# RMSNorm with swish, 16 x 1024 x 512 in fp32: in-place fp32 tiles in a deep pool, a Silu table, and stores issued from ScalarE

## The chip, the cores and the metric

The kernel runs on one core of a Trainium2 chip; the other cores are idle. The metric is device time in microseconds (us), the median over runs. A verdict of "faster" or "slower" needs a difference clear of 2%.

Engines: VectorE (DVE in the profile), ScalarE (ACT), GpSimd (POOL), SyncE (SP), and the DMA engines. `ACTq` or `SPq` is the sequencer of an engine: the part that takes instructions in order, waits for semaphores and issues DMA transfers.

## The reference

```python
# x: (16, 1024, 512) fp32, gamma: ones(512), eps: 1e-5
rms = np.sqrt(np.mean(x ** 2, axis=-1, keepdims=True) + eps)
x_norm = x / rms * gamma
return x_norm * (1.0 / (1.0 + np.exp(-x_norm)))
```

There are 16,384 rows, cut into 32 tiles of 128 partitions x 4 rows x 512 columns. A tile is 1 MiB in and 1 MiB out.

## The kernel before

Five stages of different tiles are written per step: load, squares, statistics and normalisation, sigmoid, multiply and store. A scheduler then fixes each engine's order and the semaphores.

```python
xpool = ctx.enter_context(tc.tile_pool(name="xin", bufs=6))
ypool = ctx.enter_context(tc.tile_pool(name="ybuf", bufs=5))
opool = ctx.enter_context(tc.tile_pool(name="obuf", bufs=5))
# ... load: SyncE
nc.sync.dma_start(out=x_t[:], in_=xv[t])
# ... squares: three rows on ScalarE, the fourth on VectorE; sums into ms
# ... statistics and normalisation
nc.vector.tensor_scalar_add(out=aeps[:], in0=ms[:], scalar1=eps_f)
nc.gpsimd.tensor_tensor(out=rstd[:], in0=aeps[:], in1=neg_half[:], op=ALU.pow)
for j in range(n):                          # n = 4; y is bf16
    nc.vector.scalar_tensor_tensor(out=y[:, j, :], in0=x_t[:, j, :],
        scalar=rstd[:, j : j + 1], in1=gamma_sb[:], op0=ALU.mult, op1=ALU.mult)
# ... sigmoid on ScalarE, multiply on VectorE, store from GpSimd (bf16 to fp32)
nc.scalar.activation(out=o[:], in_=y[:], func=AF.Sigmoid)
nc.vector.tensor_tensor(out=o[:], in0=y[:], in1=o[:], op=ALU.mult)
nc.gpsimd.dma_start(out=ov[t], in_=o[:])
```

## Time and profile before

| | before |
|---|---|
| time, median of 3 | 189.42 us (187.84 to 190.24) |
| DMA | 67.42 MB, mean 360 GB/s, best slices 430 |
| VectorE busy per tile | 145.1 / 32 = 4.5 us |
| ScalarE busy per tile | 122.6 / 32 = 3.8 us |

These are lines of the profile's first page for the kernel before. Part 1 gives busy time and share of the span. Part 2 cuts the span into 40 slices of 4.7 us; a digit is the busy share in tenths.

```profile
span 187.5 us, 803 instructions
## 1 busy us (share of the span) xinstructions
DVE 145.1 (77%) x257; ACT 122.6 (65%) x226; POOL 56.8 (30%) x68
## 2 busy tenths in 40 slices
DVE  0168999966998579987489976689965789999930
ACT  2478999945994289973199872399737299744520
...
DMA  6999999999999969999959999969999969887484
GB/s 171 366 421 432 367 369 418 419 426 407 388 378 402 432 257 341 395 425 423 430 231 385 383 430 421 414 231 397 383 426 425 411 199 402 318 306 285 192 309 170
```

Read the last row first. Where the DMA has work queued it moves about 425 GB/s. At that rate 67.42 MB take 159 us, so the span holds about 29 us in which the DMA was not full. The holes are of two kinds. In the first 130 us single slices drop to 257, 231 and 231 GB/s. In the last 28 us (six slices) the rate stays between 170 and 320 GB/s, while VectorE shows 9 until two slices from the end.

The next view groups instructions by line; after the bar come busy us and mean ns of one.

```profile
L105 DVE SCALAR_TENSOR_TENSOR y<-x_t,rstd,gamma_sb 128x512 bf16<-128x512 f32 x128 | 87.4, 744 | 2.3 <-POOL rstd L100 2.3
L118 ACT ACTIVATE o<-y 128x2048 bf16<-128x2048 bf16 x32 | 60.5, 1902 | 11.4 <-DVE y L105 11.1
...
L124 DVE TENSOR_TENSOR o<-y,o 128x2048 bf16<-128x2048 bf16 x32 | 39.0, 1219 | 10.4 <-ACT o L118 10.4
```

VectorE pays 4 x 744 ns for the normalisation of a tile and 1219 ns for the multiply. The waits of SyncE's DMA queue say why loads came late: a load waits until VectorE has normalised the tile that held its buffer.

```profile
engine line waited for: us in total, times, longest us
SPq L64 <- DVE y L105: 139.3, 26, 10.9
```

### The profile page before, as it was taken

How to read it: one execution, taken by the hardware profiler on the slowest of the kernel's cores; microseconds unless marked ns; L12 is line 12 of the kernel's file. 1: busy time of each engine (PE TensorE's matmuls, PEld its weight loads, DVE VectorE, ACT ScalarE, POOL GpSimd, SP SyncE). 2: the span in 40 equal slices, each digit the busy share in tenths (PEclk: the TensorE clock that was granted, in tenths of full speed). 3: DMA queues.
4: the chain of work that ended last, by engine and by line, in shares of the span. 5: the costliest groups of instructions: out<-in, count | busy, mean ns of one | idle time of the engine just before them, and what ended most of it. 6: DMA issues, size and time to landing. Idle time of an engine off the chain costs nothing.

```text
span 187.5 us, 803 instructions
## 1 busy us (share of the span) xinstructions
DVE 145.1 (77%) x257; ACT 122.6 (65%) x226; POOL 56.8 (30%) x68
## 2 busy tenths in 40 slices
DVE  0168999966998579987489976689965789999930
ACT  2478999945994289973199872399737299744520
POOL 0022651542117701236402145402132802146120
DMA  6999999999999969999959999969999969887484
GB/s 171 366 421 432 367 369 418 419 426 407 388 378 402 432 257 341 395 425 423 430 231 385 383 430 421 414 231 397 383 426 425 411 199 402 318 306 285 192 309 170
DMA packets 9365, 67.42 MB, mean 360 GB/s; under 512 B 1040, under 2 KB 1040, under 8 KB 1168
## 3 DMA queue, kind: packets, MB, share of 16 engines
q1 hardware_dynamic: 4608, 33.56, 53.6%
q0 software_dynamic: 4608, 33.56, 46.7%
q10 hardware_dynamic: 144, 0.26, 0.5%
q14 instruction: 5, 0.04, 0.1%
HBM read 33.82 MB, written 33.55 MB: 359 GB/s over the span
## 4 chain that ended last, share of the span: by engine, by line
DMA 35%; DVE 25%; issue 20%; ACT 8%; POOL 7%; POOLq 0%; SPq 0%; ACTq 0%; DVEq 0%
DMA x_t<-in_x_dram 35%; DVE y L105 19%; POOL rstd L100 5%; DVE o L124 5%; ACT o L118 5%; ACT junk_act L74 4%; POOL out_dram L125 2%; DVE junk_dve L82 1%; DVE aeps L98 0%; POOLq L174 0%; SPq L64 0%; DVE ms L82 0%; POOLq L125 0%; ACTq L74 0%; ACTq L118 0%
## 5 line engine op out<-in xcount | busy, mean ns | idle before, releaser
L105 DVE SCALAR_TENSOR_TENSOR y<-x_t,rstd,gamma_sb 128x512 bf16<-128x512 f32 x128 | 87.4, 744 | 2.3 <-POOL rstd L100 2.3
L74 ACT ACTIVATE junk_act<-x_t 128x512 bf16<-128x512 f32 x96 | 59.1, 616 | 44.2 <-DMA x_t<-in_x_dram 44.2
L118 ACT ACTIVATE o<-y 128x2048 bf16<-128x2048 bf16 x32 | 60.5, 1902 | 11.4 <-DVE y L105 11.1
L125 POOL DMA_DIRECT2D out_dram<-o x32 | 18.0, 563 | 100.3 <-DVE o L124 66.8
L124 DVE TENSOR_TENSOR o<-y,o 128x2048 bf16<-128x2048 bf16 x32 | 39.0, 1219 | 10.4 <-ACT o L118 10.4
L100 POOL TENSOR_TENSOR rstd<-aeps,neg_half 128x4 f32<-128x4 f32 x32 | 38.6, 1214 | 24.0 <-DVE aeps L98 23.7
L82 DVE CUSTOM_DVE_ANT_0 junk_dve<-x_t 128x512 bf16<-128x512 f32 x32 | 21.4, 686 | 22.0 <-DMA x_t<-in_x_dram 22.0
L74 ACT ACTIVATION_READ_ACCUMULATOR junk_act<-x_t 128x1 f32 x96 | 17.9, 187 | 0.0
L98 DVE TENSOR_SCALAR aeps<-ms 128x4 f32<-128x4 f32 x32 | 4.3, 160 | 0.0
L82 DVE DVE_READ_ACCUMULATOR2_ANT ms<- 128x1 f32 x32 | 2.6, 81 | 0.0
L74 ACT ACT_TABLE_LOAD x1 | 1.3, 1283 | 1.2 <-PEq L160 1.2
L118 ACT ACT_TABLE_LOAD x1 | 1.3, 1283 | 0.0
L50 DVE MEMSET neg_half<- 128x4 f32 x1 | 0.1, 62 | 0.8 <-PEq L160 0.8
L160 POOL MEMSET const-float32-0.0<- 128x1 f32 x1 | 0.1, 99 | 0.2 <-issue 0.2
L160 POOL MEMSET const-bfloat16-1.0<- 128x1 bf16 x1 | 0.1, 102 | 0.0
L160 POOL MEMSET const-uint8-127<- 128x1 uint8 x1 | 0.1, 102 | 0.0
L160 POOL MEMSET const-float32-1.0<- 128x1 f32 x1 | 0.1, 99 | 0.0
## 6 DMA issues: line engine op xcount, KB each, us to landing
x_t<-in_x_dram SPq DMA_DIRECT2D x32, 1024.0 KB, 8.5
out_dram<-o POOLq DMA_DIRECT2D x32, 1024.0 KB, 9.0
gamma_sb<-in_gamma_dram ACTq DMA_DIRECT2D x1, 256.0 KB, 6.8
```

The lines of the kernel that those rows point to most:

```text
L50: nc.vector.memset(neg_half[:], -0.5)
L74: nc.scalar.activation(out=junk_act[:, j, :], in_=x_t[:, j, :], func=AF.Square, scale=inv_sqrt_d, accum_out=ms[:, j : j + 1],)
L82: nc.vector.tensor_tensor_reduce(out=junk_dve[:, j - n_act_sq, :], in0=x_t[:, j, :], in1=x_t[:, j, :], scale=inv_d, scalar=0.0, op0=ALU.mu ...
L98: nc.vector.tensor_scalar_add(out=aeps[:], in0=ms[:], scalar1=eps_f)
L100: nc.gpsimd.tensor_tensor(out=rstd[:], in0=aeps[:], in1=neg_half[:], op=ALU.pow)
L105: nc.vector.scalar_tensor_tensor(out=y[:, j, :], in0=x_t[:, j, :], scalar=rstd[:, j : j + 1], in1=gamma_sb[:], op0=ALU.mult, op1=ALU.mult,)
L118: nc.scalar.activation(out=o[:], in_=y[:], func=AF.Sigmoid)
L124: nc.vector.tensor_tensor(out=o[:], in0=y[:], in1=o[:], op=ALU.mult)
L125: nc.gpsimd.dma_start(out=ov[t], in_=o[:])
L160: nc = _bacc.Bacc("TRN2", target_bir_lowering=False, num_devices=1)
```

## The change

The intent: keep one fp32 tile from load to store and work in place, which takes away the bf16 copies; replace sigmoid and multiply by one Silu on ScalarE, which takes 39 us from VectorE; give the tiles 20 buffers so that loads never wait; issue stores from ScalarE, right behind the Silu that they store. The core of the diff, with imports, asserts, renamings, the scratch pools, the squares (their scale by 1/512 moves into the statistics instruction) and the start of the load loop cut:

```diff
-    xpool = ctx.enter_context(tc.tile_pool(name="xin", bufs=6))
-    ypool = ctx.enter_context(tc.tile_pool(name="ybuf", bufs=5))
-    opool = ctx.enter_context(tc.tile_pool(name="obuf", bufs=5))
+    lead = 10
+    xpool = ctx.enter_context(tc.tile_pool(name="xbuf", bufs=20))
+    nc.scalar.preload_act_table_set("silu_and_others")
 ...
-        nc.vector.tensor_scalar_add(out=aeps[:], in0=ms[:], scalar1=eps_f)
+        nc.vector.tensor_scalar(
+            out=aeps[:], in0=ms[:], scalar1=inv_d, scalar2=eps_f,
+            op0=ALU.mult, op1=ALU.add,
+        )
 ...
-                out=y[:, j, :], in0=x_t[:, j, :], ...
+                out=x_t[:, j, :], in0=x_t[:, j, :], ...
 ...
-        nc.scalar.activation(out=o[:], in_=y[:], func=AF.Sigmoid)
-        nc.vector.tensor_tensor(out=o[:], in0=y[:], in1=o[:], op=ALU.mult)
-        nc.gpsimd.dma_start(out=ov[t], in_=o[:])
+        nc.scalar.activation(out=x_t[:], in_=x_t[:], func=AF.Silu)
+        nc.scalar.dma_start(out=ov[t], in_=xt.pop(t)[:])
 ...
+    for k in range(T + 3):
+        if k < T:
+            stats(k)
+            rstd(k)
+        if 0 <= k - 1 < T:
+            norm(k - 1)
+        if 0 <= k - 2 < T:
+            swish(k - 2)
+            store(k - 2)
+        if k + lead < T:
+            load(k + lead)
```

More of the change, by code (lines that the diff above doesn't have):

```diff
@@ L1 @@
-import math
 from contextlib import ExitStack
@@ L5 @@
 import concourse.tile as tile
-from concourse import bass_utils, mybir
+from concourse import mybir
 from concourse._compat import with_exitstack
@@ L30 @@
     n = 4
-    n_act_sq = 3 if n >= 4 else n
-    rows_per_tile = P * n
-    assert R % rows_per_tile == 0, (R, rows_per_tile)
-    T = R // rows_per_tile
+    n_act = 3
+    lead = 10
+    T = R // (P * n)
+    assert T * P * n == R, (R, n)
     xv = xf.rearrange("(t p n) d -> t p n d", p=P, n=n)
@@ L39, with load, stats @@
     consts = ctx.enter_context(tc.tile_pool(name="consts", bufs=1))
-    xpool = ctx.enter_context(tc.tile_pool(name="xin", bufs=6))
-    ypool = ctx.enter_context(tc.tile_pool(name="ybuf", bufs=5))
-    opool = ctx.enter_context(tc.tile_pool(name="obuf", bufs=5))
-    junk_pool = ctx.enter_context(tc.tile_pool(name="junk", bufs=3))
+    xpool = ctx.enter_context(tc.tile_pool(name="xbuf", bufs=20))
+    junk_a = ctx.enter_context(tc.tile_pool(name="junk_a", bufs=2))
+    junk_v = ctx.enter_context(tc.tile_pool(name="junk_v", bufs=2))
     small = ctx.enter_context(tc.tile_pool(name="small", bufs=6))
+    nc.scalar.preload_act_table_set("silu_and_others")
     gamma_sb = consts.tile([P, D], fp32)
-    nc.scalar.dma_start(out=gamma_sb[:], in_=gamma.partition_broadcast(P))
     neg_half = consts.tile([P, n], fp32)
     nc.vector.memset(neg_half[:], -0.5)
-    inv_sqrt_d = 1.0 / math.sqrt(float(D))
     inv_d = 1.0 / float(D)
     eps_f = float(eps)
-    x_tiles: dict[int, bass.AP] = {}
-    ms_tiles: dict[int, bass.AP] = {}
-    rstd_tiles: dict[int, bass.AP] = {}
-    y_tiles: dict[int, bass.AP] = {}
-    o_tiles: dict[int, bass.AP] = {}
-    def stage_load(t):
+    xt: dict[int, bass.AP] = {}
+    ms_of: dict[int, bass.AP] = {}
+    rstd_of: dict[int, bass.AP] = {}
+    def load(t):
         x_t = xpool.tile([P, n, D], fp32, name="x_t")
         nc.sync.dma_start(out=x_t[:], in_=xv[t])
-        x_tiles[t] = x_t
-    def stage_sq(t):
-        x_t = x_tiles[t]
+        xt[t] = x_t
+    def stats(t):
+        x_t = xt[t]
         ms = small.tile([P, n], fp32, name="ms")
-        junk_act = junk_pool.tile([P, n_act_sq, D], bf16, name="junk_act")
-        junk_dve = junk_pool.tile([P, max(1, n - n_act_sq), D], bf16, name="junk_dve")
         for j in range(n):
-            if j < n_act_sq:
+            if j < n_act:
+                junk = junk_a.tile([P, D], bf16, name="sq_act")
                 nc.scalar.activation(
-                    out=junk_act[:, j, :],
-                    in_=x_t[:, j, :],
-                    func=AF.Square,
-                    scale=inv_sqrt_d,
+                    out=junk[:], in_=x_t[:, j, :], func=AF.Square,
                     accum_out=ms[:, j : j + 1],
@@ L81, in stage_sq @@
             else:
+                junk = junk_v.tile([P, D], bf16, name="sq_dve")
                 nc.vector.tensor_tensor_reduce(
-                    out=junk_dve[:, j - n_act_sq, :],
-                    in0=x_t[:, j, :],
-                    in1=x_t[:, j, :],
-                    scale=inv_d,
-                    scalar=0.0,
-                    op0=ALU.mult,
-                    op1=ALU.add,
+                    out=junk[:], in0=x_t[:, j, :], in1=x_t[:, j, :],
+                    scale=1.0, scalar=0.0, op0=ALU.mult, op1=ALU.add,
@@ L90, in stage_sq, with rstd @@
                     accum_out=ms[:, j : j + 1],
                 )
-        ms_tiles[t] = ms
-    def stage_rstd_y(t):
-        ms = ms_tiles.pop(t)
-        x_t = x_tiles.pop(t)
+        ms_of[t] = ms
+    def rstd(t):
+        ms = ms_of.pop(t)
         aeps = small.tile([P, n], fp32, name="aeps")
-        nc.vector.tensor_scalar_add(out=aeps[:], in0=ms[:], scalar1=eps_f)
-        rstd = small.tile([P, n], fp32, name="rstd")
-        nc.gpsimd.tensor_tensor(
-            out=rstd[:], in0=aeps[:], in1=neg_half[:], op=ALU.pow
-        )
-        y = ypool.tile([P, n, D], bf16, name="y")
+        nc.vector.tensor_scalar(
+            out=aeps[:], in0=ms[:], scalar1=inv_d, scalar2=eps_f,
+            op0=ALU.mult, op1=ALU.add,
+        )
+        r = small.tile([P, n], fp32, name="rstd")
+        nc.gpsimd.tensor_tensor(out=r[:], in0=aeps[:], in1=neg_half[:], op=ALU.pow)
+        rstd_of[t] = r
@@ L104, in stage_rstd_y, with norm @@
+    def norm(t):
+        x_t = xt[t]
+        r = rstd_of.pop(t)
         for j in range(n):
             nc.vector.scalar_tensor_tensor(
-                out=y[:, j, :],
-                in0=x_t[:, j, :],
-                scalar=rstd[:, j : j + 1],
-                in1=gamma_sb[:],
-                op0=ALU.mult,
-                op1=ALU.mult,
-            )
-        y_tiles[t] = y
-    def stage_sigmoid(t):
-        y = y_tiles[t]
-        o = opool.tile([P, n, D], bf16, name="o")
-        nc.scalar.activation(out=o[:], in_=y[:], func=AF.Sigmoid)
-        o_tiles[t] = o
@@ L121, in stage_out @@
-    def stage_out(t):
-        y = y_tiles.pop(t)
-        o = o_tiles.pop(t)
-        nc.vector.tensor_tensor(out=o[:], in0=y[:], in1=o[:], op=ALU.mult)
-        nc.gpsimd.dma_start(out=ov[t], in_=o[:])
-    NS = 5
-    for k in range(T + NS - 1):
-        t_out = k - 4
-        t_sig = k - 3
-        t_y = k - 2
-        t_sq = k - 1
-        t_ld = k
-        if 0 <= t_out < T:
-            stage_out(t_out)
-        if 0 <= t_sig < T:
-            stage_sigmoid(t_sig)
-        if 0 <= t_y < T:
-            stage_rstd_y(t_y)
-        if 0 <= t_sq < T:
-            stage_sq(t_sq)
-        if 0 <= t_ld < T:
-            stage_load(t_ld)
+                out=x_t[:, j, :], in0=x_t[:, j, :], scalar=r[:, j : j + 1],
@@ new lines, in norm, with swish, store @@
+                in1=gamma_sb[:], op0=ALU.mult, op1=ALU.mult,
+            )
+    def swish(t):
+        x_t = xt[t]
+        nc.scalar.activation(out=x_t[:], in_=x_t[:], func=AF.Silu)
+    def store(t):
+        nc.scalar.dma_start(out=ov[t], in_=xt.pop(t)[:])
+    load(0)
+    nc.scalar.dma_start(out=gamma_sb[:], in_=gamma.partition_broadcast(P))
+    for t in range(1, lead):
+        load(t)
+    for k in range(T + 3):
[9 more added lines that the diff above has]
+            load(k + lead)
```

## The prediction

> **What bounds the kernel before.** No single engine. The DMA row of the profile moves 67.42 MB in a 187.5 us span, mean 360 GB/s; its good slices reach 418 to 432. At 425 GB/s the traffic alone would take 159 us (an estimate), so about 29 us are DMA slack. It is lost in two places. First, in the slices near 66, 94 and 122 us the rate falls to 199 to 257 GB/s: the SyncE queue waited 139 us in total for the VectorE normalisation to free one of six load buffers (view of waits), and the loads then come in bursts that start compute again (chain of waits: four DMA pieces of 9.6 to 12.4 us). Second, from 143 us on all loads are in or nearly in and VectorE is 9 to 10 tenths busy at about 3.8 us a tile, while the DMA falls to 170 to 320 GB/s. VectorE's work per tile is 4.5 us (145.1/32): 4 x 744 ns, 1219 ns multiply, 686+81+160 ns.
>
> **What the change does.** VectorE loses the 1219 ns multiply: about 3.45 us a tile (normalisation start to start is 0.66 us where undisturbed). ScalarE: sigmoid becomes Silu of the same 2048 elements. The Trainium skill (ScalarE: Activation LUTs, "What ACT_TABLE_LOAD costs") says one element per cycle for every function, fp32 and bf16 alike; the trace agrees on the step (616 ns for 512 fp32, 1902 ns for 2048 bf16: 0.84 ns an element). So 3 x 0.614 + 1.83 = 3.7 us a tile, and ScalarE becomes the slower compute engine. One table load of 1.28 us goes. Stores leave GpSimd (18 us of issue there, not critical); an issue from the SyncE queue takes 0.42 us, mostly hidden under the next square on ScalarE. The DMA bytes are unchanged; the skill (DMA: Bandwidth & Descriptors, "Issuing engines are not separate DMA queues") says the same 16 engines serve all queues, so the floor of 159 us stays.
>
> **What I expect to bind.** The built order of the changed kernel shows that loads and stores now share eight completion semaphores in turn, each transfer waiting for the one eight places before. So store 5 waits for load 10, store 7 for load 14, store 9 for load 19, store 14 for load 27, and this wait sits in ScalarE's instruction stream: ScalarE is held until loads run far ahead. Phase 1: DMA full, two loads to each store, to store 14: about 41.5 transfers of 2.47 us from 7.4 us on, i.e. until about 106 us. Phase 2: loads nearly done, 17 tiles of compute left at 3.7 us on ScalarE: about 64 us, DMA only about 0.8 full. Then the last store, 4 to 6 us. Span about 173 us; time about 173.5 us, 8 times in 10 within 164 to 180. Faster by over 2%: 0.94; within 2%: 0.05; slower: 0.01.
>
> **What would show it.** DMA slices at 410 to 430 GB/s without dips to about 100 us, then 270 to 350 until the end; ScalarE idle in the first half with store issues waiting for loads of x, and 9 to 10 tenths busy in the last third; VectorE about 112 us busy in all; GpSimd about 40 us; the chain ending in ScalarE and a store rather than VectorE.
>
> **What would make it wrong.** If the shared semaphores don't hold ScalarE, DMA stays full throughout: 161 to 165 us. If the store issue stalls ScalarE by its full 0.42 us and more, phase 2 grows by 8 us or more. If fp32 stores and loads mixed on two hardware queues run below 425 GB/s, phase 1 grows.

## The result and the profile after

| | before | after |
|---|---|---|
| time, median of 4 runs | 188.63 us (187.78 to 190.24) | 185.50 us (185.32 to 185.71) |
| ratio, 95% interval | | 0.9896 (0.9863 to 0.9929): the same within 2% |
| span | 187.5 us | 183.7 us |
| VectorE busy | 145.1 us | 110.7 us |

Ratios in the experiments differ from the ratio of the medians by at most 0.002. For the change the listed medians give 0.983, and 0.9896 can't be worked out again from the runs listed; by either figure the change is worth less than 2%.

The time lies outside the predicted 164 to 180 us, on the slow side. VectorE's busy time fell by 34 us and the time by 3. The slices of the changed kernel are 4.6 us each:

```profile
span 183.7 us, 711 instructions
...
DVE 110.7 (60%) x225; ACT 120.9 (66%) x225; POOL 32.8 (18%) x36
...
DVE  0177877777725527064443777777777777777650
ACT  2449988842572643168076987999988888888450
...
DMA  5999999999999999999999999999985555555195
GB/s 178 338 428 428 425 426 428 423 426 426 428 425 426 423 426 428 425 426 428 428 426 428 428 426 428 428 425 426 425 359 234 228 228 228 228 228 228 57 400 230
```

The DMA row has two parts. From the third to the 29th slice, to about 133 us, it is full at about 425 GB/s without a hole, as hoped. For the last ten, from about 138 us, it carries mostly 228 GB/s. That is one 1 MiB store per 4.6 us (1.049 MB / 4.62 us = 227 GB/s): all loads are done and the stores come at the pace of the computation. Within the full stretch, from the ninth to the 22nd slice, ScalarE falls again and again to between 0 and 4 tenths, and VectorE with it. They are held back there, and are short of time later.

What held them is seen in ScalarE's timeline. The columns are start, duration, engine, line and operation; the bracket is the engine's idle time before and what the profile holds to have ended it.

```profile
start us, us, engine line op out<-in xcount [idle before <-releaser]
...
69.80 0.61 ACT L68 ACTIVATE sq_act<-x_t 128x512 bf16<-128x512 f32 x1
...
76.83 0.34 ACTq L106 DMA_DIRECT2D out_dram<-x_t  x1
77.21 0.63 ACT L68 ACTIVATE sq_act<-x_t 128x512 bf16<-128x512 f32 x1 [6.71 <-DMA x_t<-in_x_dram]
...
77.84 0.61 ACT L68 ACTIVATE sq_act<-x_t 128x512 bf16<-128x512 f32 x1
```

The first square of a tile runs at 69.80 us, so that tile has landed. The second square of the same tile starts 6.71 us late, right behind the issue of a store (76.83 us). The bracket names a load, but it can't be this tile's own. It is the store's wait: the built order of the changed kernel has for this store (the store of tile 9, its tile named x_t_93)

```
58 L68 Activation sq_act_340,ms_339<-x_t_148 128x512 [waits Activation_49]
59 L106 DMACopy out_0_dram<-x_t_93 128x2048 [waits DMAHW3_49,Activation_49]
```

and semaphore DMAHW3 was last given to the load of tile 19. In the trace that load lands at 76.75 us, and the store is issued at 76.83 us. The same holds for eleven stores (4 to 12, 14 and 15): each is issued 0.07 to 0.08 us after the landing of the load that had its semaphore before. Loads from SyncE and stores from ScalarE take eight completion semaphores in turn, and a transfer waits for the one that had its semaphore before. The Trainium skill (DMA: Bandwidth & Descriptors, "Anatomy of one DMA — SWDGE (gpsimd) path") says, in a section on transfers from GpSimd: "DMA engines do not wait on semaphores", and that a wait happens on the issuing sequencer before dispatch. This trace of stores from ScalarE agrees: the wait shows as idle ScalarE. The first line below puts 41.9 us of it down to loads, 13 times. Two of these, 6.2 us at the start, are waits for a tile's own load; the other eleven, 35.7 us, are the held stores.

```profile
ACT sq_act L68 <- DMA x_t<-in_x_dram: 41.9, 13, 6.7
DVE x_t L96 <- POOL rstd L89: 37.4, 32, 1.2
```

The second line is the other loss: VectorE waits for GpSimd once per tile, 32 times, 37.4 us. The timeline of VectorE and GpSimd shows it, from 103 us on:

```profile
103.56 0.68 DVE L74 CUSTOM_DVE_ANT_0 sq_dve<-x_t 128x512 bf16<-128x512 f32 x1
...
104.17 0.17 DVE L84 TENSOR_SCALAR aeps<-ms 128x4 f32<-128x4 f32 x1
104.48 1.01 POOL L89 TENSOR_TENSOR rstd<-aeps,neg_half 128x4 f32<-128x4 f32 x1 [3.61 <-DVE aeps L84]
...
105.53 2.74 DVE L96 SCALAR_TENSOR_TENSOR x_t<-x_t,rstd,gamma_sb 128x512 f32<-128x512 f32 x4 [1.19 <-POOL rstd L89]
...
108.18 0.68 DVE L74 CUSTOM_DVE_ANT_0 sq_dve<-x_t 128x512 bf16<-128x512 f32 x1
```

One tile after another, VectorE computes the statistics of a tile (L84), GpSimd raises them to the power (L89, 1.01 us), and only then VectorE normalises the same tile (L96). It idles 1.19 us each time, and square to square the period is 108.18 - 103.56 = 4.62 us. It keeps this period to the last square at 168 us. The costs of single instructions are what the prediction took:

```profile
L96 DVE SCALAR_TENSOR_TENSOR x_t<-x_t,rstd,gamma_sb 128x512 f32<-128x512 f32 x128 | 87.8, 747 | 37.4 <-POOL rstd L89 37.4
L103 ACT ACTIVATE x_t<-x_t 128x2048 f32<-128x2048 f32 x32 | 60.8, 1901 | 15.3 <-DVE x_t L96 13.2 <-DMA out_dram<-x_t 2.1
L68 ACT ACTIVATE sq_act<-x_t 128x512 bf16<-128x512 f32 x96 | 59.0, 615 | 42.0 <-DMA x_t<-in_x_dram 41.9
L89 POOL TENSOR_TENSOR rstd<-aeps,neg_half 128x4 f32<-128x4 f32 x32 | 32.6, 1020 | 141.1 <-DVE aeps L84 141.1
```

### The profile page after: what moved, and what is told of

Read it like the earlier page. It is cut to its first block, busy times and chain, and to the rows that moved or that the text cites. A ratio compares the mean times of both kernels' runs of the same rounds, so it can differ in the third digit from the quotient of the medians.

```text
span 183.7 us, 711 instructions
## 1 busy us (share of the span) xinstructions
DVE 110.7 (60%) x225; ACT 120.9 (66%) x225; POOL 32.8 (18%) x36
## 4 chain that ended last, share of the span: by engine, by line
DMA 47%; DVE 26%; POOL 9%; issue 9%; ACT 5%; SPq 0%; ACTq 0%; POOLq 0%; DVEq 0%
DMA x_t<-in_x_dram 39%; DVE x_t L96 20%; POOL rstd L89 9%; DMA out_dram<-x_t 7%; DVE sq_dve L74 5%; ACT sq_act L68 3%; ACT x_t L103 2%; DVE aeps L84 1%; SPq L59 0%; ACTq L106 0%; POOLq L89 0%; DVE ms L74 0%; DVEq L96 0%; ACTq L68 0%
## 5 line engine op out<-in xcount | busy, mean ns | idle before, releaser
L96 DVE SCALAR_TENSOR_TENSOR x_t<-x_t,rstd,gamma_sb 128x512 f32<-128x512 f32 x128 | 87.8, 747 | 37.4 <-POOL rstd L89 37.4
L68 ACT ACTIVATE sq_act<-x_t 128x512 bf16<-128x512 f32 x96 | 59.0, 615 | 42.0 <-DMA x_t<-in_x_dram 41.9
L103 ACT ACTIVATE x_t<-x_t 128x2048 f32<-128x2048 f32 x32 | 60.8, 1901 | 15.3 <-DVE x_t L96 13.2
L89 POOL TENSOR_TENSOR rstd<-aeps,neg_half 128x4 f32<-128x4 f32 x32 | 32.6, 1020 | 141.1 <-DVE aeps L84 141.1
L74 DVE CUSTOM_DVE_ANT_0 sq_dve<-x_t 128x512 bf16<-128x512 f32 x32 | 21.9, 685 | 6.3 <-DMA x_t<-in_x_dram 6.3
L84 DVE TENSOR_SCALAR aeps<-ms 128x4 f32<-128x4 f32 x32 | 5.3, 166 | 21.8 <-ACT sq_act L68 21.8
L68 ACT ACTIVATION_READ_ACCUMULATOR sq_act<-x_t 128x1 f32 x96 | 17.9, 186 | 0.0
```

Source lines behind the costliest of these rows:

```text
L68: nc.scalar.activation(out=junk[:], in_=x_t[:, j, :], func=AF.Square, accum_out=ms[:, j : j + 1],)
L74: nc.vector.tensor_tensor_reduce(out=junk[:], in0=x_t[:, j, :], in1=x_t[:, j, :], scale=1.0, scalar=0.0, op0=ALU.mult, op1=ALU.add, accum_ ...
L84: nc.vector.tensor_scalar(out=aeps[:], in0=ms[:], scalar1=inv_d, scalar2=eps_f, op0=ALU.mult, op1=ALU.add,)
L89: nc.gpsimd.tensor_tensor(out=r[:], in0=aeps[:], in1=neg_half[:], op=ALU.pow)
L96: nc.vector.scalar_tensor_tensor(out=x_t[:, j, :], in0=x_t[:, j, :], scalar=r[:, j : j + 1], in1=gamma_sb[:], op0=ALU.mult, op1=ALU.mult,)
L103: nc.scalar.activation(out=x_t[:], in_=x_t[:], func=AF.Silu)
```

## The experiments

The account to be tested (theory A) has two parts. First, ScalarE's store issues share semaphores with loads far ahead, so the run splits: loads first, computation later. Second, in the later part VectorE's serial order sets 4.62 us a tile. Its rivals: ScalarE with its own store issues sets the late pace (B); depth is what keeps the DMA fed, so fewer buffers are worse (C); 20 buffers let the loads take the DMA first whatever the semaphores (D); stores in ScalarE's stream cost the time as such (E). Twelve kernels ran, each with three timing rounds.

### e1: VectorE's order alone

```diff
         for j in range(n):
-            nc.vector.scalar_tensor_tensor(
+            i = nc.vector.scalar_tensor_tensor(
                 out=x_t[:, j, :], in0=x_t[:, j, :], scalar=r[:, j : j + 1],
                 in1=gamma_sb[:], op0=ALU.mult, op1=ALU.mult,
             )
+            if t + 1 in aeps_ins:   # the statistics instruction of tile t + 1
+                tc.add_manual_dep(i.ins, aeps_ins[t + 1].name,
+                    mybir.DependencyInfo(mybir.DependencyClass.NoSync,
+                                         mybir.DependencyReason.DATA),
+                    reason="statistics of the next tile first")
```

The dependency fixes the order on VectorE only; it adds no semaphore.

> Only the order on VectorE changes: the four normalisations of a tile are issued after the small statistics instruction of the NEXT tile, so GpSimd raises that tile to the power while VectorE normalises. Theory A (after store 14 at 106 us VectorE's serial chain of statistics, power on GpSimd and normalisation sets 4.62 us a tile): phase 1 stays, store 14 still issues near 106 us, then ScalarE binds at about 3.7 us a tile; VectorE's wait for GpSimd falls from 37 us to under 5; time about 170 us (167 to 174). Rival B (ScalarE with its store issues sets the late pace): no change, 184 to 187 us.

Measured: 173.75 us (173.74 to 174.24), ratio 0.9197 (0.9159 to 0.9234). The same stretch of the timeline is now:

```profile
129.13 0.69 DVE L75 CUSTOM_DVE_ANT_0 sq_dve<-x_t 128x512 bf16<-128x512 f32 x1
...
130.04 0.17 DVE L85 TENSOR_SCALAR aeps<-ms 128x4 f32<-128x4 f32 x1 [0.22 <-ACT sq_act L69]
130.12 2.73 DVE L98 SCALAR_TENSOR_TENSOR x_t<-x_t,rstd,gamma_sb 128x512 f32<-128x512 f32 x4
130.36 1.38 POOL L90 TENSOR_TENSOR rstd<-aeps,neg_half 128x4 f32<-128x4 f32 x1 [2.26 <-DVE aeps L85]
...
132.77 0.68 DVE L75 CUSTOM_DVE_ANT_0 sq_dve<-x_t 128x512 bf16<-128x512 f32 x1
```

VectorE's wait for GpSimd, 37.4 us in the change, no longer stands in the view of waits. L85 is the statistics of the next tile; GpSimd's power (L90) runs beside the normalisation (L98) and takes 1.38 us there instead of 1.01, but nobody waits for it. The period is 132.77 - 129.13 = 3.64 us. Store 14 is issued at 106.38 us, as in the change (106.10 us). The slices (4.3 us each) show ScalarE at 9 tenths from the 25th slice almost to the end:

```profile
DVE  0139999761344370347075259999999999997920
ACT  2369999580717350755268089999999999999750
...
GB/s 161 333 427 429 423 427 429 425 425 429 427 425 423 427 427 427 425 427 427 427 427 427 427 427 427 427 427 427 427 425 425 427 381 305 244 274 305 309 303 274
```

Rival B falls: the late pace was VectorE's order. Stores are still held by loads as before (ScalarE waits 44.1 us for loads, 12 times). The time lies at the upper end of the range expected, and within 0.3 us of the 173.5 us that had been predicted for the change: this is the kernel that the prediction had in mind. Two phases and a late fall of the DMA rate are still there.

### e2 and e3: 12 buffers in place of 20, without and with the reorder

```diff
-    xpool = ctx.enter_context(tc.tile_pool(name="xbuf", bufs=20))
+    xpool = ctx.enter_context(tc.tile_pool(name="xbuf", bufs=12))
```

> Only the pool depth changes, 20 to 12. Loads then wait for stores one for one, and the built order has store k waiting for store k-4 in most of the program instead of for a load far ahead. VectorE's serial order stays. Theory A (loads running far ahead and held stores split the run into a DMA-bound and a compute-bound half): ScalarE's idle time for loads is spread evenly, DMA carries loads and stores to the end, about 32 x 4.62 us from 7 us on plus the last store: 166 to 170 us. Rival C (depth is what keeps the DMA fed, so fewer buffers bring back the load stalls of the kernel before): 185 us or more, with dips in the DMA rate in the first 100 us.

> Both edits. Theory A: compute could do 3.7 us a tile, DMA needs 4.94 us for a load and a store, so DMA binds from start to end: 162 to 166 us, DMA near full until the last few us, ScalarE waiting for loads throughout. Rival C: no better than the reordered kernel with 20 buffers.

Measured: e2 172.22 us (171.59 to 172.90), ratio 0.911 (0.9067 to 0.9154); e3 168.65 us (168.48 to 168.70), ratio 0.8919 (0.8885 to 0.8954). Both are a little slower than expected. For e2, the DMA row and two lines of the waits:

```profile
GB/s 162 329 427 427 429 423 427 429 425 423 425 429 429 427 421 429 431 427 423 427 431 429 425 421 429 429 423 425 431 429 427 423 425 431 425 294 221 135 360 246
```

```profile
DVE x_t L96 <- POOL rstd L89: 37.3, 32, 1.2
ACT sq_act L68 <- DMA x_t<-in_x_dram: 28.8, 7, 7.8
```

Fewer buffers are better, so rival C falls. The second block is the more telling: VectorE still waits 37.3 us for GpSimd, as in the change, and yet 13 us are gone. The wait costs only where the DMA is not what binds. In both traces one more stall of the same kind stands: ScalarE issues store 20 at 112 to 113 us and store 21 only at 126 to 127 us, 0.1 us after the landing of load 28, which had its semaphore before. How much of the distance to the floor this stall costs is not shown: e6 below has no store that waits for a load, and is only 0.8 us faster than e3.

### e4: the floor

All arithmetic was taken out; loads and stores stay. Its output is wrong, which doesn't matter for the time.

```diff
-        if k < T:
-            stats(k)
-            rstd(k)
-        if 0 <= k - 1 < T:
-            norm(k - 1)
         if 0 <= k - 2 < T:
-            swish(k - 2)
             store(k - 2)
```

> Wrong result on purpose: loads and stores alone, no arithmetic, the same pool, queues and sizes. Measures the floor that DMA sets: 159 us of traffic at 425 GB/s plus start and end, 161 to 164 us. If it comes out at 175 us or more, mixed loads and stores on two hardware queues are slower than I took them to be and all sums above are off.

Measured: 164.64 us (164.61 to 164.69).

```profile
span 162.9 us, 152 instructions
...
GB/s 156 317 431 427 429 427 429 425 429 429 427 425 431 431 423 429 427 429 427 429 431 425 429 425 431 425 431 429 427 427 427 431 425 429 429 427 427 427 429 258
```

Mixed loads and stores hold 423 to 431 GB/s from the third slice to the last but one. This is the time to compare all others with; the start (156 and 317 GB/s in the first two slices) and the end are in it.

### e5: stores with semaphores of their own, with the reorder

The kernel of e1, with

```diff
-        nc.scalar.dma_start(out=ov[t], in_=xt.pop(t)[:])
+        nc.gpsimd.dma_start(out=ov[t], in_=xt.pop(t)[:])
```

> The reordered kernel with 20 buffers (173.75 us), stores now issued from GpSimd, whose transfers have eight semaphores of their own, so that no store waits for a load. Theory A (the shared semaphores hold ScalarE until loads are far ahead): ScalarE is no longer held by store issues; stores go out as soon as they are ready, the DMA stays full to the end, 166 to 170 us. Rival D (20 buffers alone let loads take the DMA first, whatever the semaphores): no gain, 172 to 175 us, with the same fall of the DMA rate in the last fifth.

Measured: 167.05 us (166.88 to 167.12), ratio 0.8887 (0.8849 to 0.8924), with all 20 buffers. Rival D falls: depth alone does no harm. The DMA rate stays between 420 and 434 GB/s from the third slice to the last but one:

```profile
GB/s 152 320 428 426 428 424 430 420 432 420 432 422 426 428 428 426 428 426 430 426 426 430 426 426 428 426 426 428 420 434 422 428 428 424 430 424 428 428 420 52
```

But this edit changes two things, the semaphores and the issuing engine, so E was still open.

### e6: 8 buffers, with the reorder

The kernel of e1 with `bufs=8` and `lead = 6`.

> The reordered kernel with 8 buffers (6 loads ahead). With 12 buffers the last stores still waited for the last loads once, at 112 to 127 us, and 17 tiles' worth of DMA slack came at the end. Theory A: fewer loads ahead, loads and stores alternate to the end, 165.5 to 168 us, near the 164.6 us of the copy. Rival C (depth is needed): above 170 us, with dips in the DMA rate.

Measured: 167.89 us (167.75 to 168.02), ratio 0.8933 (0.8894 to 0.8971), in the expected range. (The "17 tiles' worth" in the expectation is a careless phrase for the slow last slices of e3.) Stores still come from ScalarE, and in the built order nearly every store shares its semaphore with an earlier store; none waits for a load.

### e7, e8, e10: parts of the change on the kernel before

```diff
 # e7: Silu alone
-        nc.scalar.activation(out=o[:], in_=y[:], func=AF.Sigmoid)
+        nc.scalar.activation(out=o[:], in_=y[:], func=AF.Silu)
-        nc.vector.tensor_tensor(out=o[:], in0=y[:], in1=o[:], op=ALU.mult)
 # e8: depth alone
-    xpool = ctx.enter_context(tc.tile_pool(name="xin", bufs=6))
+    xpool = ctx.enter_context(tc.tile_pool(name="xin", bufs=12))
 # e10: both
```

> The kernel before with one part of the change alone: Silu in place of sigmoid and multiply, all else (six load buffers, bf16 copies, stores from GpSimd) as it was. VectorE loses 39 us of work. If the VectorE-bound last 40 us and the late release of load buffers were the cost of before, as I read it, 168 to 176 us; if the pool of six and its load bursts were the cost, 183 us or more.

> The kernel before with another part alone: 12 load buffers in place of 6, the multiply kept. Load bursts should vanish, VectorE at 4.5 us a tile binds: 7 us + 32 x 4.5 us + the last store, about 160 us at best, limited by DMA to 166; I expect 170 to 180 us because VectorE waits still add up. If loads then run ahead of stores and VectorE is bound late, nearer 185.

> The kernel before with two parts of the change, Silu and 12 load buffers in place of 6, stores from GpSimd and bf16 copies kept. If nothing else of the change is needed, it should be DMA-bound: 166 to 169 us (Silu alone gave 171.8, depth alone 180.4). If late release of the load buffers still opens holes in the DMA, 171 us.

Measured: e7 171.78 us (171.57 to 171.98), ratio 0.9139 (0.9092 to 0.9186); e8 180.37 us (180.15 to 180.70), ratio 0.9598 (0.9556 to 0.964); e10 171.64 us (171.61 to 171.72), ratio 0.9138 (0.9103 to 0.9173).

One part of the change, Silu, by itself gave 16.5 us (188.26 to 171.78 on the same chip), far more than the whole change. That fits the reading of before, that VectorE's 4.5 us a tile and its late end were the cost. Depth alone removes the holes of the first 32 slices (143 us) and then meets VectorE, as e8's rows (slices of 4.5 us) show:

```profile
DVE  0157999999999807898970799999999999999920
...
GB/s 159 366 426 428 421 419 428 419 419 426 417 419 430 415 421 428 417 430 419 417 423 423 421 428 419 419 426 415 423 426 426 428 94 296 307 290 226 235 307 164
```

e10 missed its expectation (166 to 169 us): depth on top of Silu gave nothing. Its trace has the last load landing at about 150 us and one empty slice (37 GB/s) after it, until the last tiles' stores are ready. Its stores are issued in groups of four: the last two groups at 136.9 to 146.7 us and from 156.2 us on. All earlier stores had landed by 154.8 us, so the DMA had nothing left. In e9 (below) stores go out about every 4.9 us. Why the scheduler groups them here was not pursued. What keeping the tiles in fp32 is worth alone was not run.

### e9: one part of the change undone

The changed kernel with the one-line edit of e5 and nothing else: stores from GpSimd.

> The changed kernel with one part undone: stores from GpSimd again, with semaphores of their own; 20 buffers, VectorE's order left to the scheduler (which here puts one 0.7 us square between the statistics and the normalisation that waits for GpSimd). Theory A: no store waits for a load, so DMA at 4.94 us a tile binds and VectorE's serial chain (4 to 4.6 us) hides behind it: 166 to 170 us, nearly as good as with the reorder. If the serial chain costs by itself whatever the DMA does, 175 us or more.

Measured: 167.06 us (166.97 to 167.09), ratio 0.8892 (0.8864 to 0.8921). The move of the stores to ScalarE, with the semaphores that come with it, was worth 18 us of loss: 185.50 against 167.06 us. Loads run as far ahead here as in the change (the last is issued at 107.2 us, against 101.5), so loads far ahead do no harm while no store waits for them. VectorE's order is not quite that of the change: its wait for GpSimd is 11.8 us instead of 37.4. The full reorder adds nothing (e5: 167.05 us).

### e11 and e12: the same engines and depth, other pairs on the semaphores

This separates the last two readings. Stores stay on ScalarE and the pool at 20. A dependency that fixes order only puts load t behind store t-8 when semaphores are dealt out. Loads are also written 6 tiles ahead instead of 10. For most of the program store k then shares its semaphore with store k-4, and load t with load t-4. The build adds every wait that is needed; none was taken out by hand.

```diff
-    lead = 10
+    lead = 6
 ...
-        nc.sync.dma_start(out=x_t[:], in_=xv[t])
+        i = nc.sync.dma_start(out=x_t[:], in_=xv[t])
+        if t - 8 in store_ins:
+            tc.add_manual_dep(i.ins, store_ins[t - 8].name,
+                mybir.DependencyInfo(mybir.DependencyClass.NoSync,
+                                     mybir.DependencyReason.DATA),
+                reason="place in the order only")
 ...
-        nc.scalar.dma_start(out=ov[t], in_=xt.pop(t)[:])
+        store_ins[t] = nc.scalar.dma_start(out=ov[t], in_=xt.pop(t)[:]).ins
```

> The changed kernel with 20 buffers, stores still from ScalarE, VectorE's order as in the change, the same eight shared semaphores. Only the place of each load in the order in which semaphores are dealt out changes (load t after store t-8), so that store k shares its semaphore with store k-4 and load t with load t-4; no wait is taken out by hand. Theory A (what holds ScalarE is that its stores share semaphores with loads far ahead): 166 to 170 us, like stores from GpSimd. Rival E (stores in ScalarE's stream cost the time, or 20 buffers do, whatever they share): 180 us or more.

> The paired semaphores and VectorE's reorder together. If DMA binds in both, the reorder adds nothing more: 166 to 168 us, within 1% of the paired kernel alone. If VectorE's serial chain still costs in the paired kernel, this one is faster by more than 1%.

Measured: e11 165.92 us (165.82 to 166.13), ratio 0.8875 (0.8833 to 0.8916); e12, which adds the reorder of e1, 165.97 us (165.92 to 166.06), ratio 0.8876 (0.8842 to 0.8911). Both give the right result. They have the lowest medians of the correct kernels, but their ratios overlap with those of e5 and e9, so no order among these four is shown. e11's median is 1.3 us above that of the copy of e4, which ran on another chip. Its page (slices of 4.1 us) and two lines of its waits:

```profile
span 164.2 us, 730 instructions
...
DVE  0157777887777777887777777887777768776710
ACT  3266998887897777777897778775788777779440
...
GB/s 151 330 425 427 427 425 427 429 423 425 425 431 425 427 429 425 425 431 425 431 425 425 431 425 427 427 425 427 427 423 431 427 431 423 425 431 425 429 371 202
```

```profile
DVE x_t L105 <- POOL rstd L98: 37.4, 32, 1.2
...
ACT sq_act L77 <- DMA x_t<-in_x_dram: 18.1, 13, 5.0
```

Rival E falls too: stores are issued from ScalarE, the pool is 20 deep, and VectorE waits 37.4 us for GpSimd exactly as in the change. What differs is which transfers share a semaphore, and with it how far ahead loads are issued. (Loads are then also limited to four at a time, as each waits for the one four places before. That this limit is not what helps is seen in e9, where loads run far ahead.) No store is now held: each is issued at least 3.4 us after the landing of the store that had its semaphore before. ScalarE's wait for loads falls from 41.9 to 18.1 us, both engines work evenly from start to end, and the computation keeps step with the transfers.

### All together

Times are medians in us. The runs were made on several chips, on which the kernel before took 187.0 to 188.9 us, so differences under about 1% between rows mean little.

| stores and pool | scheduler's VectorE order | reordered |
|---|---|---|
| ScalarE, 20 buffers, semaphores as dealt out (the change) | 185.50 | 173.75 (e1) |
| ScalarE, 12 buffers | 172.22 (e2) | 168.65 (e3) |
| ScalarE, 8 buffers | not run | 167.89 (e6) |
| GpSimd, 20 buffers | 167.06 (e9) | 167.05 (e5) |
| ScalarE, 20 buffers, paired semaphores | 165.92 (e11) | 165.97 (e12) |
| copy only (e4) | 164.64 | |

The two losses are not a sum. The reorder alone recovers 11.8 us, other partners on the semaphores alone 19.6, both together 19.5. That is because VectorE's serial order, 4.62 us a tile, is still faster than the DMA's need for a load and a store, 2 x 1.049 MB / 425 GB/s = 4.94 us. It costs only in a phase in which the loads are already done, and that phase is made by the semaphores.

## Why the prediction was wrong, point by point

- **What binds before: right as far as tested.** e7 and e8 show that both named costs are real: VectorE's work (16 us) and the six load buffers (8 us). (A slip in the text: the three slices named fall to 257, 231 and 231 GB/s; the 199 belongs to the slice near 150 us.)
- **The shared semaphores hold ScalarE: right.** It was read from the built order. Store 14 was put at about 106 us; it was issued at 106.10 us, 0.07 us after its partner, load 27, landed. That the number is so close is in part luck: the sum as written, 7.4 + 41.5 x 2.47, gives 109.9 us, and the trace has 28 loads and 12 stores landed by then, 40 transfers. e11 shows the mechanism by changing the partners and the lead of the loads, with stores still on ScalarE.
- **DMA full to about 100 us: right, and short.** It stayed full to about 133 us, since the last loads and queued stores filled it.
- **The step that failed: "17 tiles of compute left at 3.7 us on ScalarE: about 64 us".** From store 14 to store 31 (issued at 178.91 us) it took 72.8 us. With 106.1 before and 4.8 us for the last store that gives the span of 183.7 us, against about 173 predicted. The 3.7 us of ScalarE were right: e1 runs at 3.64. But VectorE was put at "about 3.45 us a tile" from its busy time alone (measured 110.7 / 32 = 3.46). It needs 4.62 us, because the scheduler had put the statistics of a tile directly before the normalisation of the same tile, with GpSimd's power between them. (The 72.8 us are less than 17 x 4.62 us as VectorE was already starting on tile 16 when store 14 went out: 15 normalisations were left. Stores 16 to 20 follow each other at 3.6 to 3.8 us while ScalarE catches up; from store 21, at 133 us, to store 28 they come every 4.62 us.) That order stood in the same built program from which the semaphores had been read. The prediction says nothing of it.
- **Following from it, also wrong:** ScalarE was not 9 tenths busy at the end, the late DMA rate was 228 GB/s and not 270 to 350, and the late chain runs through VectorE and GpSimd.
- **GpSimd busy about 40 us: a little off,** 32.8 us.
- **Silu costs what sigmoid did: right.** 1901 ns in fp32 against 1902 ns in bf16, as the Trainium skill has it (ScalarE: Activation LUTs, "What ACT_TABLE_LOAD costs").
- **A store issue hides under the next square: right where it doesn't wait.** It takes 338 ns, and e1 reaches 3.64 us a tile with it.
- **The floor: right.** 161 to 165 us was said for a DMA full throughout; the copy took 164.64 us and e11 165.92 us.

## What to carry to other kernels

Read the built order of every engine, not the busy times: ask of each wait what it shares a semaphore with and which engine's stream it stands in, and of each hop to another engine whether other work lies between request and use. Here a store's wait held everything behind it on the engine that issued it, so stores that shared semaphores with far-ahead loads turned a deep pool into a phase of loading and a phase of computing. And try the parts of a change alone: here one line undone, or two order hints, was worth more than the whole change.

## What the Trainium skill lacked or had wrong

- DMA: Bandwidth & Descriptors, "Rules for kernel authors", says that spreading transfers over SyncE, ScalarE and GpSimd only saves sequencer issue time. For bandwidth that held. But moving the stores' issue from ScalarE to GpSimd, which also gave them semaphores of their own, took the time from 185.50 to 167.06 us (e9). The rule doesn't mention that a wait before an issue stands in the issuing engine's stream (6.71 us of idle ScalarE before store 9).
- The same page, "Why a DMA increments its semaphore by 16 and not by 1", asks for one semaphore per slot in flight. It doesn't say what sharing one between streams that run at different distances costs when the sharing is safe: 185.50 against 165.92 us (e11).
- The same page, "Where 436 GB/s comes from", says that for transfers between HBM and SBUF the HBM side (about 358 GB/s) binds; it works this out as 716 GB/s over two cores, and doesn't say there that a core alone isn't held to it. On one core with the others idle, mixed loads and stores ran at 423 to 431 GB/s (e4), in line with the single-core measurement of 425 that the same page has.
- The same page, "Issuing engine by pattern", says that hardware-generated transfers (SyncE, ScalarE) are generally faster, and not in what. In bandwidth no difference shows here: with stores from GpSimd the DMA held 420 to 434 GB/s (e5), with stores from ScalarE 423 to 431 (e11).
- No page gives the time of GpSimd's power of 128 x 4 elements: 1.01 us alone, 1.38 us beside VectorE's normalisation (both in the timelines above, of the change and of e1).
